# A transformer trunk on one core: when weight units are split, and where the pre-norm's mean stands, in the first blocks of each phase

## The chip, the cores and the metric

The kernel runs on one core of one Trainium2 chip. The metric is the device time of one execution in microseconds (us), as the median of several runs. The kernel before takes 2264.59 us (three runs, 2262.05 to 2264.63).

## The reference

It computes one layer of a decoder trunk on 288 tokens: 256 of a prompt and 8 times 4 of samples that continue a stored state. The width is 2048, the FFN's inner width 5632.

```python
x = x + 0.5 * rmsnorm(swiglu(rmsnorm(x, g[0]), ffn1_w_in, ffn1_w_out), g[1])
m, sg, sh = hybrid_mixer(rmsnorm(x, g[2]), mix_w_in, ..., s_gla, s_hgrn)
x = x + rmsnorm(m, g[3])
x = x + 0.5 * rmsnorm(swiglu(rmsnorm(x, g[4]), ffn2_w_in, ffn2_w_out), g[5])
```

In the mixer one projection gives `q, k, v, a_lr, r` of a gated linear attention (GLA, four heads) and the inputs of a second recurrence (HGRN2, eight heads). The decay of GLA comes from the low-rank part: `log_sigmoid(a_lr @ gla_w_up + gla_b) / 16`. Both recurrences are `S_t = diag(a_t) S_{t-1} + k_t^T v_t`, `o_t = q_t S_t`, worked out in chunks: scores `q k^T` with the decays inside, and the states.

## The kernel before, in words

**Layout.** Activations lie transposed, features on the 128 partitions and 288 tokens in the free dimension: x is 16 tiles `x0` to `x15` of 128x288. The program is there twice, once as it runs and once more in a branch that these inputs don't take; only the first copy is spoken of.

**Precision.** Every large product is made of three matmuls on numbers split into a high and a low part: high x by high weight, low x by high weight, high x by low weight (lines 555 to 557). ScalarE makes the high part of x (`xh`) with the norm's gain in it, VectorE the low part (`xl`, line 273).

**Weights.** They are read in units of 512 KB, numbered through the whole program in the order of their use. A unit is loaded by SyncE's queue into one of three buffers (`raw269` is unit 269's), and then *split*: ScalarE copies it to `wh` (line 101), VectorE subtracts to `wl` (line 102). That is `part()`. There are four buffers for split units, so a unit can be split when TensorE has finished the one four places before; some units at the head of a phase have two more buffers. A raw buffer is asked for again once its unit is split. `W.ahead(most)` splits as many units as there is room for, `most` at most. `W.behind`, if it is set, names instructions of which the next call's instructions are to come after in the order of the schedule (`issue_after`). What stands on an engine is set by that order, and each engine runs its own in sequence.

**Blocks.** `block()` makes a 128x4 by 2048 product: four column tiles of 128 rows of output (`qk0_0` to `qk0_3`) in four banks, over 16 rows k of x. Two rows make a unit, so a block has eight. After each unit but the last `W.ahead(most)` is called. The last unit is taken column by column, so that the banks come free one after the other, and each is emptied by `evac`. `tick(k)`, called behind each row k, places other work.

**Heads of phases.** The first block of a phase runs while the previous phase's norm is still being applied to x. `update(k)` makes `y[k]` (line 528), `x[k]` (529) and the two parts of x for one k. It is called by `tick0` of class `PreNorm`, eight rows ahead in the mixer and the second FFN. For the first column of such a block the first four rows are instead made from the old x and the unscaled update (class `Fill`): TensorE takes them ahead of the sum of squares; `scaled()` and `total()` put them together in `fsum` (lines 514 and 517). The second block, `v0` or the first `up`, has `tick1`: it squares x tiles (ScalarE) and adds them to `acc` (VectorE, line 417), and at k == 9 sets up the new norm: TensorE's `pre` (the mean, a product with a constant, line 444), a root on ScalarE, a reciprocal on VectorE (446), and what waited for it (`late`): in the mixer the scaling of `q_g`, `k_g`. The block's evacuations multiply by the reciprocal `rt`.

On TensorE `pre` stands in the middle of row 10 of that second block.

The mixer's blocks come in the order `qk0` (units 264 to 271), `v0` (272 to 279), `qk1` (280 to 287), `v1`. Between `v0` and `qk1` stands the head of the decay: `a_lr` (32 small matmuls, lines 1601 to 1605) and `gla_decay`, which multiplies by the gate's weights (`zp`, line 1612), and takes logarithms. The transposes of v's four tiles (`tp_v`, from `y8` to `y11`, line 939) are `turns`, taken one at a time by `tick` in `qk1`; `later` is a list of functions of which each tick takes one. The scan's scores (`sc`) then need the decayed keys `k_g`.

Of the kernel before, what the change touches and what calls it, by code (L numbers as in the profile page):

```python
# [13 lines left out]
ALU = mybir.AluOpType  # L14
# [129 lines left out]
def trunk(ctx, tc, x_prompt, x_sample, state_gla, state_hgrn, norm_gains, f1_in, f1_out, f2_in, f2_out,  # L144
# [3 lines left out]
    V, S, G, PE = nc.vector, nc.scalar, nc.gpsimd, nc.tensor  # L148
# [16 lines left out]
    def order(ins, before):  # L165
        tc.add_manual_dep(ins, before.name, mybir.DependencyInfo(mybir.DependencyClass.NoSync,
                                                                 mybir.DependencyReason.DATA), reason="act table")
# [16 lines left out]
    def mmtile(name):  # L184
        return mmp.tile([P, 512], F32, name=name, tag="mm")

    def auxtile(name):
        return aux.tile([P, 512], F32, name=name, tag="aux")


    W = Weights(tc, rawp, hlp)
# [132 lines left out]
    def x_copy(k, tp):  # L324
        return S.activation(x[k], tp, AF.Copy).ins if k % 2 else V.tensor_copy(x[k], tp).ins
# [4 lines left out]
    def after(ins, f, *args):  # L330
        with ExitStack() as es:
            for i in (*chain["pin"], *ins):
                es.enter_context(tc.issue_after(i))
            chain["pin"] = f(*args)
        return chain["pin"]
# [73 lines left out]
    def sq_add(src, k, pool=0, late=KT, n=KT):  # L409

        sq = acc if k == 0 else sqp.tile([P, T], F32, name="sq", tag="sq")
        if k < late:
            ins = S.activation(sq, src, AF.Square).ins
        else:
            ins = V.tensor_tensor(sq, src, src, op=ALU.mult).ins
        if 0 < k < n:
            (G if k < pool else V).tensor_tensor(acc, acc, sq, op=ALU.add)
        return sq, ins
# [21 lines left out]
    def rstd(dst, parts, name):  # L440

        ms = auxtile(name)
        for i, part in enumerate(parts):
            PE.matmul(ms[:, 0:T], onesD, part, start=i == 0, stop=i == len(parts) - 1)
        act(dst, ms[:, 0:T], AF.Sqrt, bias=epst)
        return V.reciprocal(dst, dst).ins

    class PreNorm:
# [6 lines left out]
        def tick0(self, k):  # L455
            if k + self.ahead < KT:
                self.split = self.update(k + self.ahead)

        def tick1(self, k):
            if k < 8:  # L460
                with tc.issue_after(self.split[0]), tc.issue_after(self.split[1]):
                    for j in (2 * k, 2 * k + 1):
                        sq_add(x[j], j)
            if k == 9:
                ins = rstd(rt, (acc,), self.name)

                behind = [G.memset(gate[:, 0:1], 0.0).ins, V.tensor_copy(gate[:, 1:2], epst).ins,
                          S.activation(gate[:, 2:3], epst, AF.Copy).ins]
                with ExitStack() as es:
                    for i in behind:  # L470
                        order(i, ins)
                        es.enter_context(tc.issue_after(i))
                    for f in self.late:
                        f()

    class Fill:
# [37 lines left out]
            V.tensor_tensor(self.sum, self.sum, self.scale[:, 0:T], op=ALU.mult)  # L514

        def total(self, ps):
            V.tensor_tensor(self.sum, self.sum, ps, op=ALU.add)
            return self.sum

    def post_norm(gcol, gnext, lasts, name, fill):  # L520
# [25 lines left out]
    def block(name, nk, rhs, evac, width=512, tick=None, tail=1, hold=False, most=99, fill=None, made=None):  # L546

        nf, per = width // P, 1024 // width
        nu = nk // per
        ps = [mmtile(f"{name}_{f}") for f in range(nf)]  # L550
        ws = [W.next() for _ in range(EARLY // per)] if fill else []

        def mm3(dst, w, f, k, parts, start, stop):
            c = (k % per) * width + f * P
            yield lambda: PE.matmul(dst, w[0][:, c:c + P], parts[0], start=start, stop=False)  # L555
            yield lambda: PE.matmul(dst, w[0][:, c:c + P], parts[1], start=False, stop=False)  # L556
            yield lambda: PE.matmul(dst, w[1][:, c:c + P], parts[0], start=False, stop=stop)  # L557

        def row(w, k):

            rows = [list(mm3(ps[f][:, 0:T], w, f, k, rhs(k), k == 0, False)) for f in range(nf)]
            made.extend(row[0]().ins for row in rows)
            if k == 0:
                after(made[-1:], second)
                after((), lambda: (x_copy(1, tps[1]), x_copy(0, tps[0])))
            with tc.issue_after(first.last if k == 0 else made[-1]):
                made.extend(row[i]().ins for i in (1, 2) for row in rows)

        def mm(w, f, k):
            if made is not None and k < 3:  # L570
                if f == 0:
                    row(w, k)
            elif not fill or f or k >= EARLY:
                for ready in mm3(ps[f][:, 0:T], w, f, k, rhs(k), k == 0, k == nk - 1):
                    ins = ready().ins
                    if made is not None:
                        made.append(ins)

        if fill:
            fill.products(lambda dst, k, parts, stop: mm3(dst, ws[k // per], 0, k, parts, k == 0, stop), ps[0][:, 0:T])  # L580
        for u in range(nu - tail):
            w = ws.pop(0) if ws else W.next()
            for k in range(u * per, (u + 1) * per):
                for f in range(nf):
                    mm(w, f, k)
                if tick is not None:
                    tick(k)
            W.ahead(most)
            if fill and u == 5:
                fill.scaled()  # L590
        ws = [W.next() for _ in range(tail)]
        for f in range(nf):
            for k in range((nu - tail) * per, nk):
                mm(ws[k // per - (nu - tail)], f, k)
            evac(f, fill.total(ps[f][:, 0:T]) if fill and f == 0 else ps[f][:, 0:T])
        for k in range((nu - tail) * per, nk):
            if tick is not None:
                tick(k)
        if not hold:
            W.ahead()  # L600
# [227 lines left out]
    def mixer(pn, border):  # L828
        with ExitStack() as mx:
# [103 lines left out]
            def group_tiles(nm):  # L933
                return {n: gp.tile([P, 2, T], F32, name=f"{n}_{nm}", tag=n) for n in ("q", "k", "f")}
# [40 lines left out]
            def log_sigmoid(out, z):  # L975

                e = tmp.tile([P, T], F32, name="ls", tag="ls")
                S.activation(e, z, AF.Abs)
                act(e, e, AF.Exp, scale=-1.0)
                act(e, e, AF.Ln, bias=1.0)  # L980
                V.scalar_tensor_tensor(out, z, 0.0, e, op0=ALU.min, op1=ALU.subtract)
# [579 lines left out]
            gens, later = [], []  # L1561
# [46 lines left out]
            def gla_decay(d, g):  # L1608
                for f in range(2):
                    a = 2 * g + f  # L1610
                    zp = auxtile("zp")
                    PE.matmul(zp[:, 0:T], aw[g][:, f * P:(f + 1) * P], alr, start=True, stop=True)
                    z = tmp.tile([P, T], F32, name="z", tag="z")
                    V.tensor_scalar(z, zp[:, 0:T], prm[:, 96 + a:97 + a], None, op0=ALU.add)
                    log_sigmoid(d["f"][:, f, :] if blockwise else z, z)
                    if not blockwise:
                        act(d["f"][:, f, :], z, AF.Exp, scale=1.0 / 16.0)
# [24 lines left out]
            for g in range(2):  # L1642
                d = group_tiles(f"g{g}")
                block(f"qk{g}", KT, xrhs, ev_gla(d, g == 0), tick=tick if g else pn.tick0, most=99 if g else 1,
                      fill=None if g else border.fill)
                if g == 0:
                    scan_pool()
                vt = vtiles(f"g{g}")
                if g == 0:
                    block("v0", KT, xrhs, ev_v(*vt), tick=pn.tick1)  # L1650
                    lower_bounds()
                    a_lr()
                    gla_decay(d, g)
                else:
                    gla_decay(d, g)
                    block("v1", KT, xrhs, ev_v(*vt), tick=tick)
                gens.append((g, (block_scan if blockwise else scan)(d, *vt, True, 4 * g, state_gla[0][:, 2 * g:2 * g + 2],
                                     sgp[0, 0, 2 * g:2 * g + 2], sgs[0][:, 2 * g:2 * g + 2]), True))
# [92 lines left out]
    u, border = ffn(1, lambda k: hg1[:, k:k + 1], 2, pn, first)  # L1751
    u, border = mixer(PreNorm("pre2", u, UPDATED), border)
# [45 lines left out]
```

## Time and profile before

| | |
|---|---|
| three runs | 2264.59 us median, 2262.05 to 2264.63 |
| the profiled execution, own time | 2262.32 us |
| its span | 2260.6 us |
| granted TensorE clock, mean | 0.999 |
| TensorE busy | 2247.0 us, 99% |
| VectorE busy | 1363.3 us, 60% |
| ScalarE busy | 1005.0 us, 44% |
| GpSimd busy | 78.3 us, 3% |

The span is the profiled time from the first to the last instruction; the execution's own time is 1.7 us longer. All times within the program are counted from the span's start. Matmuls are pipelined: the end of one is modelled, and the next starts before it.

### The profile page before, as it was taken

The page shows a single profiled execution, that of the slowest core. Times are in us where ns is not written, and L with a number is a line of the kernel's source. Part 1 is how long each engine was busy: PE and PEld are TensorE (multiplying, and loading weights), DVE is VectorE, ACT ScalarE, POOL GpSimd, SP SyncE. Part 2 cuts the span into 40 slices and gives each one's busy share as a digit, 9 for nine tenths or more (in the row PEclk, how much of TensorE's full clock was granted, in tenths as well). Part 3 has the DMA queues.
Part 4 walks back from the last instruction along what each step waited for, and adds up shares of the span by engine and source line. Part 5 has one row for each costly group of instructions (what it writes and reads, how often), then busy time and mean ns, then how long its engine had stood idle before and what let it go on. Part 6 is the DMA issues. An engine that isn't in the chain of part 4 may idle for free.

```text
span 2260.6 us, 41346 instructions
## 1 busy us (share of the span) xinstructions
PE 2247.0 (99%) x17075; PEld 2228.9 (99%) x17075; DVE 1363.3 (60%) x2166; ACT 1005.0 (44%) x1509; POOL 78.3 (3%) x143
## 2 busy tenths in 40 slices
PE   9999999999999999999999999999999999999998
PEld 9999999999999999999999999999999999999998
DVE  7545545554565468778788755844555455545545
ACT  6443333333334344545566644544333343333345
POOL 0000000000000003022110000100000000000000
PEclk9999999999999999999999999999999999999999
DMA  6555555555555555466565664555555555555553
GB/s 212 167 168 167 162 167 167 168 163 166 166 168 179 169 166 161 128 216 201 172 170 166 175 185 123 169 168 167 164 165 167 168 160 167 164 165 166 168 163 113
DMA packets 207330, 377.94 MB, mean 167 GB/s; under 512 B 15410, under 2 KB 40992, under 8 KB 207136
## 3 DMA queue, kind: packets, MB, share of 16 engines
q1 hardware_dynamic: 198832, 356.83, 52.8%
q0 software_dynamic: 5984, 17.97, 2.6%
q8 instruction: 135, 2.21, 0.4%
q10 hardware_dynamic: 2320, 0.44, 0.1%
q14 instruction: 59, 0.48, 0.1%
HBM read 363.39 MB, written 11.80 MB: 166 GB/s over the span
## 4 chain that ended last, share of the span: by engine, by line
PE 96%; DVE 2%; DMA 1%; ACT 1%; issue 1%; SPq 0%; DVEq 0%; ACTq 0%
PE gate L555 10%; PE gate L556 10%; PE gate L557 10%; PE out L556 8%; PE out L557 8%; PE out L555 8%; PE up L557 8%; PE up L555 8%; PE up L556 8%; PE mo L557 2%; PE mo L555 2%; PE mo L556 1%; PE hfq L555 1%; PE hfq L556 1%; PE hfq L557 1%; PE hi L555 1%
## 5 line engine op out<-in xcount | busy, mean ns | idle before, releaser
L102 DVE TENSOR_TENSOR wl<-raw,wh 128x1024 fp32r<-128x1024 f32 (+1 forms) x674 | 821.7, 1220 | 646.1 <-ACT wh L101 643.7
L101 ACT ACTIVATE wh<-raw 128x1024 fp32r<-128x1024 f32 (+1 forms) x673 | 710.7, 1057 | 1056.0 <-PE gate L556 313.0
L556 PE MATMUL gate<-xl,wh 128*128 128x288 f32 x1660 | 488.2, 295 | 0.1
L555 PE MATMUL gate<-xh,wh 128*128 128x288 f32 x1660 | 488.1, 297 | 0.2 <-ACT xh L272 0.2
L557 PE MATMUL gate<-xh,wl 128*128 128x288 f32 x1660 | 487.9, 295 | 0.0
L556 PE MATMUL out<-hl,wh 128*128 128x288 f32 x1408 | 416.2, 296 | 0.0
L555 PE MATMUL out<-hh,wh 128*128 128x288 f32 x1408 | 415.7, 295 | 0.0
L557 PE MATMUL up<-xh,wl 128*128 128x288 f32 x1408 | 415.5, 295 | 0.0
L557 PE MATMUL out<-hh,wl 128*128 128x288 f32 x1408 | 415.3, 295 | 0.0
L556 PE MATMUL up<-xl,wh 128*128 128x288 f32 x1408 | 415.3, 295 | 0.0
L555 PE MATMUL up<-xh,wh 128*128 128x288 f32 x1408 | 415.0, 295 | 0.0
L556 PEld LDWEIGHTS gate<-xl,wh 128*128 128x128 f32 x1660 | 311.7, 188 | 1.2 <-DVE xl L273 0.7
L555 PEld LDWEIGHTS gate<-xh,wh 128*128 128x128 f32 x1660 | 310.4, 188 | 1.2 <-ACT xh L272 0.7
L557 PEld LDWEIGHTS gate<-xh,wl 128*128 128x128 f32 x1660 | 311.3, 188 | 0.0
L555 PEld LDWEIGHTS out<-hh,wh 128*128 128x128 f32 x1408 | 265.0, 188 | 0.0
L557 PEld LDWEIGHTS out<-hh,wl 128*128 128x128 f32 x1408 | 264.9, 188 | 0.0
L556 PEld LDWEIGHTS out<-hl,wh 128*128 128x128 f32 x1408 | 264.8, 188 | 0.0
L557 PEld LDWEIGHTS up<-xh,wl 128*128 128x128 f32 x1408 | 264.5, 188 | 0.1
L556 PEld LDWEIGHTS up<-xl,wh 128*128 128x128 f32 x1408 | 264.4, 188 | 0.1
L555 PEld LDWEIGHTS up<-xh,wh 128*128 128x128 f32 x1408 | 264.3, 188 | 0.1
L704 DVE TENSOR_TENSOR y<-out,y 128x288 f32<-128x288 f32 x287 | 121.0, 452 | 103.7 <-PE out L557 100.8
L555 PE MATMUL hfq<-xh,wh 128*128 128x288 f32 x256 | 78.0, 305 | 0.0
(383 smaller groups left out, 2403.4 us busy)
## 6 DMA issues: line engine op xcount, KB each, us to landing
raw<-in_ffn_w_in_dram SPq DMA_DIRECT2D x351, 512.0 KB, 3.7
raw<-in_ffn_w_out_dram SPq DMA_DIRECT2D x176, 512.0 KB, 3.7
raw<-in_mix_w_in_dram SPq DMA_DIRECT2D x64, 512.0 KB, 3.7
raw<-in_mix_w_in_dram SPq DMA_DIRECT2D x96, 256.0 KB, 3.5
raw<-in_mix_w_out_dram SPq DMA_DIRECT2D x32, 512.0 KB, 3.7
out_dram<-s POOLq DMA_DIRECT2D x32, 256.0 KB, 3.5
s<-in_state_gla_dram POOLq DMA_DIRECT2D x16, 256.0 KB, 4.8
s<-in_state_hgrn_dram POOLq DMA_DIRECT2D x16, 256.0 KB, 4.5
```

The source lines that it names most:

```text
L101: i1 = self.nc.scalar.activation(h[:, c], raw[:, c], AF.Copy).ins
L102: i2 = self.nc.vector.tensor_tensor(l[:, c], raw[:, c], h[:, c].bitcast(F32), op=ALU.subtract).ins
L555: yield lambda: PE.matmul(dst, w[0][:, c:c + P], parts[0], start=start, stop=False)
L556: yield lambda: PE.matmul(dst, w[0][:, c:c + P], parts[1], start=False, stop=False)
L557: yield lambda: PE.matmul(dst, w[1][:, c:c + P], parts[0], start=False, stop=stop)
L704: V.tensor_tensor(y[k], ps, y[k], op=ALU.add)
```

## The change

It has five edits.

1. In `tick0`, for the phases that update x ahead (`made is None`), the next splits come behind ScalarE's instruction for the high part of the x tile that was last updated.
2. In `tick1` the mean is set up at k == 11 instead of k == 9.
3. `total()` makes the next splits come behind the first column's sum.
4. In a block with `fill`, the splits behind the first and the seventh unit are left out, and behind the others one unit is split, also where `most` was larger. Other blocks are as before.
5. In the mixer `gla_decay(d, 0)` does not follow `a_lr` directly but is put on `later` as the third of three functions, the first two of which do nothing: it is called at the third tick of `qk1`.

```diff
--- before.py
+++ after.py
@@ -455,13 +455,15 @@
         def tick0(self, k):
             if k + self.ahead < KT:
                 self.split = self.update(k + self.ahead)
+                if self.made is None:
+                    W.behind = self.split[:1]
 
         def tick1(self, k):
             if k < 8:
                 with tc.issue_after(self.split[0]), tc.issue_after(self.split[1]):
                     for j in (2 * k, 2 * k + 1):
                         sq_add(x[j], j)
-            if k == 9:
+            if k == 11:
                 ins = rstd(rt, (acc,), self.name)
 
                 behind = [G.memset(gate[:, 0:1], 0.0).ins, V.tensor_copy(gate[:, 1:2], epst).ins,
@@ -514,7 +516,7 @@
             V.tensor_tensor(self.sum, self.sum, self.scale[:, 0:T], op=ALU.mult)
 
         def total(self, ps):
-            V.tensor_tensor(self.sum, self.sum, ps, op=ALU.add)
+            W.behind = [V.tensor_tensor(self.sum, self.sum, ps, op=ALU.add).ins]
             return self.sum
 
     def post_norm(gcol, gnext, lasts, name, fill):
@@ -585,7 +587,10 @@
                     mm(w, f, k)
                 if tick is not None:
                     tick(k)
-            W.ahead(most)
+            if not fill:
+                W.ahead(most)
+            elif 0 < u < nu - tail - 1:
+                W.ahead(1)
             if fill and u == 5:
                 fill.scaled()
         ws = [W.next() for _ in range(tail)]
@@ -1650,7 +1655,7 @@
                     block("v0", KT, xrhs, ev_v(*vt), tick=pn.tick1)
                     lower_bounds()
                     a_lr()
-                    gla_decay(d, g)
+                    later.append([lambda: None, lambda: None, lambda d=d: gla_decay(d, 0)])
                 else:
                     gla_decay(d, g)
                     block("v1", KT, xrhs, ev_v(*vt), tick=tick)
```

`fsum`'s lines and others behind the first edit have numbers higher by 2 to 5 in the changed kernel (line 517 is 519, 1594 is 1599).

On VectorE, at the end of `qk0` and the start of `v0`, the rows from the split of 272 to that of 275 are these before (`wl` is a low part, `fsum` the first column's sum, `q_g0` and `k_g0` what the columns are copied to):

```order
L102 TENSOR_TENSOR wl272_9489<-raw272_9360,wh272_9488 128x1024
L273 SCALAR_TENSOR_TENSOR xl14_160<-x14_112,prm_94,xh14_144 128x288
L273 SCALAR_TENSOR_TENSOR xl15_161<-x15_113,prm_94,xh15_145 128x288
L102 TENSOR_TENSOR wl273_9519<-raw273_9392,wh273_9518 128x1024
L514 TENSOR_TENSOR fsum_9524<-fsum_9524,post1s_9278 128x288
L102 TENSOR_TENSOR wl274_9552<-raw274_9430,wh274_9551 128x1024
L517 TENSOR_TENSOR fsum_9524<-fsum_9524,qk0_0_9265 128x288
L1594 COPY q_g0_9262<-qk0_1_9266 128x288
L1594 COPY q_g0_9262<-fsum_9524 128x288
L1594 COPY k_g0_9263<-qk0_2_9267 128x288
L1594 COPY k_g0_9263<-qk0_3_9268 128x288
L102 TENSOR_TENSOR wl275_9587<-raw275_9492,wh275_9586 128x1024
```

and in the changed kernel:

```order
L102 TENSOR_TENSOR wl271_9459<-raw271_9237,wh271_9458 128x1024
L102 TENSOR_TENSOR wl272_9489<-raw272_9386,wh272_9488 128x1024
L516 TENSOR_TENSOR fsum_9524<-fsum_9524,post1s_9278 128x288
L417 TENSOR_TENSOR acc_164<-acc_164,sq_9619 128x288
L519 TENSOR_TENSOR fsum_9524<-fsum_9524,qk0_0_9265 128x288
L1599 COPY q_g0_9262<-qk0_1_9266 128x288
L102 TENSOR_TENSOR wl273_9519<-raw273_9424,wh273_9518 128x1024
L1599 COPY q_g0_9262<-fsum_9524 128x288
L1599 COPY k_g0_9263<-qk0_2_9267 128x288
L1599 COPY k_g0_9263<-qk0_3_9268 128x288
L102 TENSOR_TENSOR wl274_9581<-raw274_9462,wh274_9580 128x1024
L102 TENSOR_TENSOR wl275_9587<-raw275_9492,wh275_9586 128x1024
```

The split of 273 now stands between the copy of `qk0_1` and those of `fsum` and `qk0_2`, where it stood ahead of all of them, and that of 274 moves behind the four copies. Further up, the splits of 269, 270 and 271 move from behind x8, x11 and x13 to behind x12, x15 and `xl15`.

On TensorE, at the end of `v0`, where `v0_3` is the block's last column, the order before is

```order
L556 MATMUL v0_3_9605<-xl15_161,wh279_9768 128x288
L557 MATMUL v0_3_9605<-xh15_145,wl279_9769 128x288
L1605 MATMUL a_lr_9975<-x0_98,a32_9254 32x288
L1605 MATMUL a_lr_9975<-x1_99,a32_9254 32x288
L1605 MATMUL a_lr_9975<-x2_100,a32_9254 32x288
L1605 MATMUL a_lr_9975<-x3_101,a32_9254 32x288
```

and in the changed kernel

```order
L558 MATMUL v0_3_9605<-xl15_161,wh279_9768 128x288
L559 MATMUL v0_3_9605<-xh15_145,wl279_9769 128x288
L944 MATMUL tp_v_10024<-ident_84,y8_122 128x128 x2
L945 MATMUL tp_v_10024<-ident_84,v3_9930 96x128
L944 MATMUL tp_v_10051<-ident_84,y9_123 128x128 x2
L945 MATMUL tp_v_10051<-ident_84,v3_9939 96x128
L1610 MATMUL a_lr_9975<-x0_98,a32_9254 32x288
L1610 MATMUL a_lr_9975<-x1_99,a32_9254 32x288
```

The transposes of `y8` and `y9` and of their `v3` (the sample tokens' part) stood behind the second and the third row of `qk1` and are now ahead of `a_lr`. `zp`, which had five matmuls of `qk1` between `a_lr` and itself, now stands behind three rows of `qk1`, 36 matmuls. `pre` moves from the middle of row 10 of `v0` to the end of its row 11, 17 matmuls later; 48 matmuls of `v0` are left behind it.

On VectorE, behind the mean, the rows from the split of 280 on are these before (`gate`, `sel`, `hgain` and `a32` are small set-ups of the mixer, `rt` the reciprocal):

```order
L102 TENSOR_TENSOR wl280_9856<-raw280_9686,wh280_9855 128x1024
L446 RECIPROCAL rt_162<-rt_162 128x288
L467 COPY gate_93<-epst_91 128x1
L917 TENSOR_TENSOR sel_9253<-ident_84 128x32
L922 TENSOR_SCALAR hgain_9252<-prm_94 128x3
L1595 SCALAR_TENSOR_TENSOR q_g0_9262<-q_g0_9262,rt_162 128x288
```

and in the changed kernel:

```order
L102 TENSOR_TENSOR wl280_9800<-raw280_9686,wh280_9799 128x1024
L102 TENSOR_TENSOR wl281_9887<-raw281_9729,wh281_9886 128x1024
L446 RECIPROCAL rt_162<-rt_162 128x288
L469 COPY gate_93<-epst_91 128x1
L922 TENSOR_TENSOR sel_9253<-ident_84 128x32
L927 TENSOR_SCALAR hgain_9252<-prm_94 128x3
L1600 SCALAR_TENSOR_TENSOR q_g0_9262<-q_g0_9262,rt_162 128x288
```

The split of 281 now stands ahead of the reciprocal. In both kernels the other scalings of `q_g0` and `k_g0` follow, then a split (of 281 before, of 282 in the changed kernel), and then `y8`, the scaling of v's first column (line 960).

## Rows read from the trace of the kernel before

**Rows 1.** Page, the span and the busy line

```profile
span 2260.6 us, 41346 instructions
...
PE 2247.0 (99%) x17075; PEld 2228.9 (99%) x17075; DVE 1363.3 (60%) x2166; ACT 1005.0 (44%) x1509; POOL 78.3 (3%) x143
```

**Rows 2.** Timeline, TensorE, mixer's head: start us, us, instruction, [idle before <-releaser]

```profile
874.92 0.56 PE L555 MATMUL qk<-xh,wh 128*128 128x288 f32 x3
...
887.62 0.40 PE L555 MATMUL v<-xh,wh 128*128 128x288 f32 x1 [0.81 <-DVE fsum L517]
...
889.95 0.61 PE L555 MATMUL v<-xh,wh 128*128 128x288 f32 x1 [1.01 <-DVE k_g L1594]
...
893.23 0.30 PE L555 MATMUL v<-xh,wh 128*128 128x288 f32 x1
...
905.55 0.29 PE L555 MATMUL v<-xh,wh 128*128 128x288 f32 x1
906.47 0.73 PE L444 MATMUL pre<-acc,onesD 128*128 128x288 f32 x2 [0.64 <-DVE acc L417]
```

**Rows 3.** Windows: window, us, busy PE, PEld, DVE, ACT, POOL, granted clock, DMA share, GB/s

```profile
890.00:893.30 3.30, 3.30 (x14) 3.30 (x15) 2.22 (x4) 0.73 (x1) 0.00 (x0) 0.52 0.32 71
```

**Rows 4.** Timeline, second FFN's head: TensorE at the mean, VectorE at a copy

```profile
1443.36 0.72 PE L444 MATMUL pre<-acc,onesD 128*128 128x288 f32 x2 [0.47 <-DVE acc L417]
...
1427.65 0.30 DVE L629 COPY g<-fsum 128x288 f32<-128x288 f32 x1
```

**Rows 5.** Timeline, VectorE in qk0 and behind it

```profile
867.03 0.50 DVE L529 SCALAR_TENSOR_TENSOR x<-y,hg,x 128x288 f32<-128x288 f32 x1
...
868.88 1.22 DVE L102 TENSOR_TENSOR wl<-raw,wh 128x1024 fp32r<-128x1024 f32 x1
...
870.02 0.95 DVE L273 SCALAR_TENSOR_TENSOR xl<-x,prm,xh 128x288 fp32r<-128x288 f32 x2
870.88 0.52 DVE L529 SCALAR_TENSOR_TENSOR x<-y,hg,x 128x288 f32<-128x288 f32 x1
871.31 0.82 DVE L528 TENSOR_TENSOR y<-y,post1s 128x288 f32<-128x288 f32 x2
...
887.85 1.69 DVE L1594 COPY q_g<-fsum 128x288 f32<-128x288 f32 x1
```

**Rows 6.** Page, DMA issues: count, KB each, median us to landing

```profile
raw<-in_mix_w_in_dram SPq DMA_DIRECT2D x64, 512.0 KB, 3.7
```

**Rows 7.** Chain that ended last: start us, us, what

```profile
878.20 6.58 DMA raw<-in_mix_w_in_dram
```

**Rows 8.** Timeline, GpSimd at the mixer's head

```profile
872.08 4.95 POOL L1295 DMA_DIRECT2D s<-in_state_gla_dram  x7 [12.42 <-PE qk L556]
...
883.91 3.85 POOL L906 DMA_DIRECT2D y<-in_gla_w_gate_up_dram  x8
888.01 0.76 POOL L911 MEMSET Dg<- 128x768 f32 x1
```

**Rows 9.** Timeline, ScalarE behind the mean

```profile
907.24 0.50 ACT L179 ACTIVATE rt<-pre,epst 128x288 f32<-128x288 f32 x1 [0.61 <-PE pre L444]
```

**Rows 10.** Timeline, VectorE behind the mean

```profile
907.80 1.95 DVE L446 RECIPROCAL rt<-rt 128x288 f32<-128x288 f32 x1
...
911.86 1.22 DVE L102 TENSOR_TENSOR wl<-raw,wh 128x1024 fp32r<-128x1024 f32 x1
...
913.46 0.42 DVE L960 TENSOR_TENSOR y<-v,rt 128x256 f32<-128x256 f32 x1 [0.26 <-PE v L557]
```

**Rows 11.** Timeline, TensorE behind v0 and at the first scores

```profile
915.75 2.15 PE L1605 MATMUL a_lr<-x,a 128*32 128x288 f32 x32
...
918.59 1.19 PE L1612 MATMUL zp<-y,y 128*128 128x288 f32 x4
...
936.18 0.59 PE L1393 MATMUL sc<-q_g,k_g 128*128 128x256 f32 x2
```

**Rows 12.** Timeline, VectorE at the decayed keys

```profile
930.18 0.75 DVE L1348 TENSOR_TENSOR k_g<-k_g,f_g 128x576 f32<-128x576 f32 x1
```

## The prediction

> **What bounds the kernel now.** I began with the page's busy line: TensorE is busy for 2247.0 of 2260.6 us [rows 1]. So only time that TensorE loses can be won. Then I asked for the list of TensorE's waits. Apart from the start and one later score they lie in two places: the head of the mixer (the blocks `qk0` and `v0`, 854 to 916 us) and the up block at the head of the second FFN (1443 us).
>
> In the mixer's head one matmul of 288 columns follows another every 0.1325 us when nothing is late: 93 steps from 893.23 to 905.55 [rows 2]. From 874.92 (row k=10 of `qk0`) to the mean's matmul at 906.47 there are 199 matmuls, so 26.4 us of work in 31.55 us: 5.2 us are lost. The reader finds most of it in the same rows: 0.81 us for the total of the first tile, 1.01 for the copies of `qk0` out of their banks, and 0.64 for `acc`, the sum of squares; a smaller wait for the last x tiles is not shown. Each such figure is 0.16 short, since a matmul's modelled end lies 0.295 after its start. Behind the third wait the rows of `v0` stand 0.24 apart, and the stretch 890 to 893.3 has a granted clock of 0.52, the 1.2 GHz level, with 14 matmuls in 3.30 us where 1.86 would do [rows 3]: 1.44 us that the waits cost afterwards. In the second FFN's head only the wait for `acc` is left, 0.47 + 0.16 = 0.6 us [rows 4]. In the first FFN's head the mean waits for nothing (the list has nothing there). All that this change can win is thus 5.2 + 0.6 = 5.8 us, 0.26% of 2264.59. The kernel's three runs lie 2.6 us apart; about 0.2% (4.5 us) is what a measurement can tell from no change.
>
> **Part 1: the splits move behind x's tiles.** VectorE is the late engine in `qk0`. A tile of x costs it 1.22 us (0.36 for y, 0.43 each for x and `xl`), a weight split 1.14 [rows 5]. Before, units 269 to 273 are split between the tiles. Now 269 stands behind x12. I count its place from x7's update at 867.0: twelve steps of 0.43 and four of 0.36 give 873.6, so the split of 269 ends at 874.8, in time for k=10 at 874.9. Five steps and three y's later that of 270 ends at 879.2, and TensorE, which now runs four columns' high products first, needs it at 874.9 + 2 x 1.59 + 8 x 0.1325 = 879.1: 0.2 us lost with the semaphore (0 to 0.3). The split of 271 ends at 881.2, wanted at 881.3. `qk0` ends at 884.7; the wait for the last x tiles is gone.
>
> What is late next is the DMA. There are three raw slots, so the request of unit 272 waits for the split of 269, now 874.9 instead of 870.1, and that of 273 for the split of 270, 879.3. A unit lands in 3.7 us as a rule [rows 6] but took 6.58 [rows 7] when the mixer's states, requested at 872 to 877 [rows 8], were being loaded beside it. For 272 I take 5.8 (the states are in the queue throughout), so 880.7, split by 883.0; the sum, the total and the copy of column 1 follow by 884.6. So the total comes when TensorE comes to the second column of `v0`: the 0.81 is gone too. For 273 I take 4.6, between the ends, because most of the state bytes are in by then: 883.9, high part 885.0, low part 886.2. The changed order puts this split ahead of the copies of `fsum` and of column 2. They take 0.4 each, so column 2's bank is free at 887.1. TensorE is at the fourth column of `v0` (which needs that bank) ten matmuls after 884.7, at 886.0: a wait of 1.1, with the restart 1.2 us. With 3.7 for the DMA it is 0.2, with 6.58 it is 3.1. The half clock behind 889.95 goes if this wait stands alone, as I assume.
>
> **Part 2: the mean two rows later.** The squares are summed as before, by 906.4 at the latest (the mean started then); the mean's place is 17 matmuls later, so the waits of 0.64 and 0.47 go. But what hangs on the mean is 2.3 us later against the end of the block. Call the start of the mean's matmul t. ScalarE must first split unit 281 (the order puts it ahead of the root; its buffer is free at t): t + 0.3 to 1.3. Then the root, which before began 0.77 after the mean [rows 2, 9]. VectorE's split of 281 runs to t + 2.5 and holds the reciprocal. From the reciprocal's start to the next split before lie 4.06 us [rows 10]; that split is 1.14, then comes `y8`: t + 7.7 to 8.1. TensorE reaches the transposes of `y8`, which the new order puts ahead of `a_lr`, at t + 0.35 + 48 x 0.1325 = t + 6.7. Before, `y8` was begun at 913.46 [rows 10] and its transposes came far behind `a_lr` at 915.75 [rows 11]. With `v3`, `y9` and `v3` still to follow, `a_lr` starts at t + 9.0 rather than t + 7.4: a new wait of 1.6 us (1.3 to 2.0, by how soon ScalarE gets the buffer).
>
> The heads of the two FFNs have no transposes there. The first evacuation of the up block is reached by the same sum at t + 7.2, and the next block's second column asks for that bank at about t + 7.1: 0.2 us in each (0 to 0.5).
>
> **Part 3: the first decay in the next block.** `zp` began at 918.59, 0.7 us after `a_lr` (915.75, 2.15 long), and now comes behind its third row, 36 matmuls or 4.8 us in. The decayed keys were ready at 930.93 and the scores ran at 936.18 [rows 11, 12]: 5.2 us of cover. The move takes 4.0 of it, one split more that now stands in that chain 1.14, and the scores' turn comes 0.5 sooner as two transposes moved ahead: a wait of about 0.5 (0 to 1.1).
>
> **At nothing.** The splits left out behind the first and seventh units are made by the block's last call, which is unchanged: as many splits and requests in all. The splits of `fill2x` in the first FFN move behind its products; nobody reads them for 790 us.
>
> **The sum.** Won 5.8; new 0.2 + 1.2 + 1.6 + 0.5 + 0.2 + 0.2 = 3.9. That is -1.9 us on the profiled run, 2262.32 (span 2260.6): 2260.4. The median of the runs shown is 2.3 above that run, so I forecast 2264.6 - 1.9 = 2262.7.
>
> **Rivals.** *The clock drops behind a new wait.* The trace shows it behind 0.81 and 1.01 close together, not behind 0.64 alone. At 1.44 each, one drop gives 2264.1, two 2265.6. The Trainium skill ("TensorE: Matmul & The Clock Gate", section "What's actually happening") says that the throttled state is the default and activity releases it; the 0.52 behind the two waits agrees.
>
> *The copy of `fsum` stays slow.* At 887.85 it took 1.69 us [rows 5], its like in the second FFN 0.30 [rows 4]. GpSimd was then running its sets of `Dg` and their neighbours [rows 8]; at 886.2 it will still be issuing the eight loads before them (883.91 to 887.76). Beside loads the trace shows no such copy, so its price lies between 0.3 and 1.7. I take 0.4, since nothing is shown to block it there; 1.7 puts the wait at 2.5 and the time at 2264.0. The Trainium skill ("SBUF — State Buffer", section "Who interferes with whom") holds that a copy in a two-port mode and a GpSimd instruction shut each other out, whichever comes second waiting. By that rule a load being issued could hold the copy as the sets did; the slow copy beside them agrees, and for loads no row here decides.
>
> *Slower: the decay chain.* If the keys come 5 us after the scores' turn instead of 0.5, because ScalarE takes logarithms and splits in a worse order, the wait of 5 and a half clock add 5.9: 2268.6, and 2269.1 from 0.5 us more. It turns the change into a loss from a wait of 2.4 on. Against it stands the 5.2 of cover.
>
> *Nothing new waits.* The DMA in 3.7 us and a score chain without loss leave 0.2 + 1.6: -4.0, 2260.6. If the transposes are covered too it is 2258.8, which is more than 0.2%.
>
> *The change doesn't do what it says:* the freed VectorE time only moves the waits to 273's load, 3.1 rather than 1.2 us: 2264.6.
>
> **How the numbers follow.** Forecast 0.42; clock 0.18; slow copy 0.13; waits only moved 0.09; nothing new waits 0.10, of which 0.07 beyond 0.2%; decay chain 0.08, of which 0.07 beyond. So faster 0.07, same 0.86, slower 0.07. The range leaves out the two ends: from -4.3 (the best case without the transposes' full 1.6) to +2.2 (two clock drops and the slow copy), 2260.3 to 2266.8.
>
> **What would show it.** Right: no wait for x's high part or for `acc` in the heads; one wait of TensorE of about a microsecond for the copy of column 2 near 886 us; a wait of 1.3 to 1.6 for `y8` behind `v0`; a granted clock of 1 all through. Wrong: the load of unit 273 landing before 883 or after 885, a copy of `fsum` over a microsecond, a clock of 0.5 behind either wait, or a wait for the scores over 1.1 us.

## The result, and the profile after

The changed kernel takes 2264.69 us (median of 22 runs, 2261.70 to 2268.52), the kernel before 2261.32 (22 runs, 2258.77 to 2264.63, the three shown above among them). The ratio is 1.0016, 95% interval 1.0009 to 1.0022: it is slower by 3.4 us, or 2 to 5. A gain of 1.9 was forecast. The profiled execution after took 2264.74, close to its median; the one before, 2262.32, is 1.0 above its median.

The page of the changed kernel, which answers to [rows 1]:

```profile
span 2263.0 us, 41353 instructions
...
PE 2247.3 (99%) x17075; PEld 2228.8 (98%) x17075; DVE 1362.1 (60%) x2166; ACT 1006.4 (44%) x1509; POOL 78.5 (3%) x143
```

The same work, 2.4 us more of span. TensorE's timeline in the mixer's head, the answer to [rows 2]:

```profile
885.97 0.29 PE L557 MATMUL v<-xh,wh 128*128 128x288 f32 x1
888.93 0.40 PE L557 MATMUL v<-xh,wh 128*128 128x288 f32 x1 [2.67 <-DVE k_g L1599]
...
893.21 0.30 PE L557 MATMUL v<-xh,wh 128*128 128x288 f32 x1
...
908.32 0.65 PE L444 MATMUL pre<-acc,onesD 128*128 128x288 f32 x2
...
916.29 0.44 PE L944 MATMUL tp_v<-ident,y 128*128 128x128 f32 x2 [0.96 <-DVE y L965]
...
938.25 0.70 PE L1398 MATMUL sc<-q_g,k_g 128*128 128x256 f32 x2 [0.99 <-DVE k_g L1353]
```

The reader finds the three new waits at the three places named in the prediction: the copy of a column of `qk0` ahead of `v0_3`, the scaling `y8` ahead of its transposes, the decayed keys ahead of the scores. The mean at 908.32 waits for nothing, and neither does the one in the second FFN. The first wait is more than twice as long as forecast. The granted clock in the stretches around it:

```profile
874.90:884.70 9.80, 9.72 (x72) 9.31 (x71) 9.23 (x17) 5.35 (x9) 9.80 (x25) 1.00 0.95 290
884.70:889.80 5.10, 2.43 (x18) 2.19 (x17) 3.53 (x6) 3.44 (x4) 5.10 (x12) 1.00 0.67 186
889.80:893.20 3.40, 3.40 (x16) 3.40 (x15) 2.88 (x5) 1.43 (x3) 1.75 (x4) 0.50 0.77 242
```

In the third stretch it is 0.50, as in [rows 3], behind one long wait instead of two short ones. The chain of waits says what came late first; the columns are start, length, what:

```profile
879.32 5.84 DMA raw<-in_mix_w_in_dram
885.27 1.07 ACT wh L101
```

and VectorE's timeline goes on from there, and shows the places of the two later waits:

```profile
886.36 1.23 DVE L102 TENSOR_TENSOR wl<-raw,wh 128x1024 fp32r<-128x1024 f32 x1 [1.57 <-ACT wh L101]
887.50 1.02 DVE L1599 COPY q_g<-fsum 128x288 f32<-128x288 f32 x1
888.44 0.80 DVE L1599 COPY k_g<-qk 128x288 f32<-128x288 f32 x2
...
914.68 1.22 DVE L102 TENSOR_TENSOR wl<-raw,wh 128x1024 fp32r<-128x1024 f32 x1
915.82 0.41 DVE L965 TENSOR_TENSOR y<-v,rt 128x256 f32<-128x256 f32 x1
...
936.31 1.22 DVE L102 TENSOR_TENSOR wl<-raw,wh 128x1024 fp32r<-128x1024 f32 x1
937.45 0.75 DVE L1353 TENSOR_TENSOR k_g<-k_g,f_g 128x576 f32<-128x576 f32 x1
```

Three times a weight split stands directly ahead of the instruction for which TensorE waits. The first of them itself waits 1.57 us, since its unit, 273, landed at 885.2.

### The profile page after: what moved, and what is told of

Same layout as the page of the kernel before. It is cut to its first block, busy times and chain, and to the rows that moved or that the text cites. A ratio compares the mean times of both kernels' runs of the same rounds, so it can differ in the third digit from the quotient of the medians.

```text
span 2263.0 us, 41353 instructions
## 1 busy us (share of the span) xinstructions
PE 2247.3 (99%) x17075; PEld 2228.8 (98%) x17075; DVE 1362.1 (60%) x2166; ACT 1006.4 (44%) x1509; POOL 78.5 (3%) x143
## 4 chain that ended last, share of the span: by engine, by line
PE 95%; DVE 3%; DMA 1%; ACT 0%; issue 0%; ACTq 0%; SPq 0%; DVEq 0%
PE gate L557 10%; PE gate L559 10%; PE gate L558 10%; PE out L558 8%; PE up L559 8%; PE up L557 8%; PE out L559 8%; PE up L558 8%; PE out L557 8%; PE mo L559 2%; PE mo L557 1%; PE mo L558 1%; PE hfq L557 1%; PE hfq L558 1%; PE hfq L559 1%; PE v L557 1%
```

## The experiments

Each ratio is to the kernel before, timed beside it on the same chip.

| run | median, us | ratio, 95% interval |
|---|---|---|
| splits alone | 2264.37 | 1.0015, 1.0005 to 1.0024 |
| mean alone | 2261.94 | 1.0005, 0.9996 to 1.0014 |
| decay alone | 2261.93 | 1.0006, 0.9997 to 1.0015 |
| changed, 273 behind the copies | 2260.80 | 1.0002, 0.9993 to 1.0011 |
| splits alone, 273 behind the copies | 2261.44 | 1.0004, 0.9995 to 1.0013 |
| the same, mean at k == 10 | 2258.42 | 0.9989, 0.9980 to 0.9998 |
| changed, mean at k == 10 | 2263.94 | 1.0012, 1.0002 to 1.0021 |
| changed, decay behind `a_lr` | 2265.68 | 1.0017, 1.0008 to 1.0026 |
| changed, state loads held back | 2261.84 | 1.0005, 0.9996 to 1.0014 |
| 273 behind the copies, k == 10, state loads held back | 2258.71 | 0.9989, 0.9980 to 0.9998 |

### Each part by itself

The splits alone, against the changed kernel:

```diff
-            if k == 11:
+            if k == 9:
...
-                    later.append([lambda: None, lambda: None, lambda d=d: gla_decay(d, 0)])
+                    gla_decay(d, g)
```

> Only the edits to the splits (1, 3 and 4); the mean at k == 9 and the decay behind a_lr as before. Theory A (the loss is a sum of three new waits, one of each part, of which this part only moves time): VectorE's split of 273 still stands ahead of the copies that free qk0's banks and waits for its load, TensorE loses 2 to 3 us at the fourth column of v0, the clock is half from 889.8 to 893.2, and the wait for acc stays (0.6); 0 to 1 us slower than before. Rival B (the whole loss comes from the splits): 2.5 to 4 us slower. Rival C (the splits win and the other two parts lose): 1 to 3 us faster.

TensorE's timeline of that run, and its windows around a second fall of the clock (of which more in the last section):

```profile
886.03 0.40 PE L557 MATMUL v<-xh,wh 128*128 128x288 f32 x1 [0.70 <-DVE fsum L519]
...
889.69 0.47 PE L557 MATMUL v<-xh,wh 128*128 128x288 f32 x1 [2.48 <-DVE k_g L1599]
...
907.07 0.72 PE L444 MATMUL pre<-acc,onesD 128*128 128x288 f32 x2 [0.47 <-DVE acc L417]
```

```profile
1394.00:1398.40 4.40, 4.40 (x39) 4.40 (x38) 2.51 (x4) 1.77 (x4) 0.00 (x0) 1.00 0.26 101
1398.50:1401.80 3.30, 3.30 (x16) 3.30 (x16) 0.18 (x1) 0.24 (x1) 0.00 (x0) 0.50 0.55 164
```

It measured 3.4 us slower than before, by the ratio (1.1 to 5.4): rival B of that run. Each wait is as theory A has it, but the sum isn't: the splits alone are as slow as the whole change. Of what this profile lost against the first one of before, 2.3 us lie in the second FFN's head: the second fall of the clock, which no other trace has, and 0.97 instead of 0.47 for `acc`. Theory A compared with the first profile of before, and what follows shows that this profile was no fair base.

The mean alone and the decay alone, against before:

```diff
-            if k == 9:
+            if k == 11:
```

```diff
-                    gla_decay(d, g)
+                    later.append([lambda: None, lambda: None, lambda d=d: gla_decay(d, 0)])
```

> Only the mean at k == 11. Theory A: the waits for acc (0.64 in the mixer, 0.47 in the second FFN) go and no transposes stand ahead of a_lr, since it is the decay's move that puts them there: 0.5 to 1.6 us faster. Rival B: the later reciprocal makes TensorE wait for y8 or for the first evacuation all the same: same to 1.5 us slower, with a wait of over 0.5 us at a_lr or in qk1.

> Only the decay moved to qk1's third tick. Theory A: two rows' time of cover is gone, so the first scores wait 0 to 1 us for the decayed keys; the transposes of y8 stand ahead of a_lr but y8 is there in time, since the mean is early: 0 to 1.2 us slower. Rival B (the scores' wait in the changed kernel came from the later mean alone): no wait at the scores, 0.2 us either way.

The mean alone has a new wait at `zp`, for VectorE's scaling of `a_lr`:

```profile
916.73 1.24 PE L1612 MATMUL zp<-y,y 128*128 128x288 f32 x4 [1.89 <-DVE y L1606]
```

So rival B holds for it: `acc`'s two waits are gone, and 1.9 us come back one step later. With the decay alone:

```profile
886.73 0.40 PE L555 MATMUL v<-xh,wh 128*128 128x288 f32 x1 [1.24 <-DVE fsum L517]
...
903.16 0.72 PE L444 MATMUL pre<-acc,onesD 128*128 128x288 f32 x2 [0.64 <-DVE acc L417]
...
934.26 0.70 PE L1393 MATMUL sc<-q_g,k_g 128*128 128x256 f32 x2 [0.75 <-DVE k_g L1348]
```

The scores wait 0.75 with the mean early, so theory A holds. Both times lie within what can be told from no change. But these two kernels have before's order in `qk0` and the first rows of `v0`, and neither shows the waits and the half clock of [rows 2, 3].

### The same kernels once more

Both kernels as they are, for another profile of each; nothing is edited.

> The kernel before, a second look at the mixer's head. Theory A (what it lost there in its first profile, 0.8 and 1.0 us and the half clock, was large by chance, since the runs with the mean alone and with the decay alone have the same order up to the mean and lost 0.2 and 1.4): 0.2 to 2 us lost between the second half of qk0 and v0's fourth row, and no half clock. Rival B (4 us are lost there as a rule): both waits and the half clock come again.

> The changed kernel, a second look. Theory A: the wait at v0's fourth column comes again with 2.3 to 3 us and the half clock behind it, the transposes wait 0.9 to 1.2, the first scores 0.8 to 1.1, and the HGRN scores near 1109 us about 1. Rival B (these are chance as well): two of the four differ by over 0.7 us from the first look.

The kernel before, second profile: TensorE's timeline, ScalarE's around the split of 273 (its copy to `wh`, then the high parts of the last x tiles), and the row of the chain for the load of 274:

```profile
884.85 0.80 PE L555 MATMUL qk<-xh,wh 128*128 128x288 f32 x4 [2.30 <-ACT xh L272]
...
890.10 0.40 PE L555 MATMUL v<-xh,wh 128*128 128x288 f32 x1 [0.46 <-DVE fsum L517]
...
906.25 0.72 PE L444 MATMUL pre<-acc,onesD 128*128 128x288 f32 x2 [0.64 <-DVE acc L417]
```

```profile
883.32 1.06 ACT L101 ACTIVATE wh<-raw 128x1024 fp32r<-128x1024 f32 x1 [4.91 <-DMA raw<-in_mix_w_in_dram]
884.28 0.95 ACT L272 ACTIVATE xh<-x,prm 128x288 fp32r<-128x288 f32 x2
```

```profile
879.05 8.21 DMA raw<-in_mix_w_in_dram
```

The changed kernel, second profile:

```profile
888.01 0.40 PE L557 MATMUL v<-xh,wh 128*128 128x288 f32 x1 [1.41 <-DVE k_g L1599]
...
913.83 0.44 PE L944 MATMUL tp_v<-ident,y 128*128 128x128 f32 x2 [0.96 <-DVE y L965]
```

For the kernel before neither theory holds whole. Its long wait stood in another place (the last x tiles, 2.30) and had no half clock: the load of 273 took 7.75 us, ScalarE's split of it waited 4.91 for that, and the last two high parts stood behind the split. So a split that waits for its load holds up TensorE in this order too, on ScalarE. The load of 274, at 8.21, made the wait of 0.46. For the changed kernel rival B holds: the waits at the transposes and the scores came again (0.96 and 1.01), but the first was 1.41 without a half clock, and the one near 1109 us, which the first profile had with 1.07, was absent. To compare, the same stretch of matmuls in every trace, from one in `qk0` to the 116th of `v0` (in row 9), ahead of any mean; its 247 steps need 247 x 0.1325 = 32.73 us:

| trace | first start | last start | lost, us | half clock |
|---|---|---|---|---|
| before | 866.78 | 904.09 | 4.6 | yes |
| before, second profile | 867.62 | 903.86 | 3.5 | no |
| mean alone | 867.35 | 901.06 | 1.0 | no |
| decay alone | 866.03 | 900.78 | 2.0 | no |
| changed | 866.72 | 904.48 | 5.0 | yes |
| changed, second profile | 867.04 | 902.03 | 2.3 | no |
| splits alone | 866.67 | 905.25 | 5.9 | yes |
| changed, decay behind `a_lr` | 867.36 | 905.94 | 5.9 | yes |
| changed, mean at k == 10 | 866.43 | 904.78 | 5.6 | yes |
| changed, 273 behind the copies | 865.58 | 900.67 | 2.4 | no |
| splits alone, 273 behind the copies | 867.20 | 900.70 | 0.8 | no |
| the same, k == 10 | 867.13 | 902.25 | 2.4 | no |
| changed, state loads held back | 867.66 | 902.06 | 1.7 | no |
| 273 behind, k == 10, held back | 867.42 | 901.02 | 0.9 | no |

The first four have before's order in this stretch: 2.8 on average, from 1.0 to 4.6. The next five have the changed order: 4.9, four of them over 5. So the splits' part costs about 2.1 there, where the prediction had it win; with such a spread in so few traces the 2.1 is rough. (The four profiled executions lie 0.3 us below their kernels' medians on average, the five 0.6, so the choice of profiles does not make the difference.)

### The split of 273 behind the copies

```diff
-            elif 0 < u < nu - tail - 1:
+            elif 0 < u < nu - tail - 2:
...
-                        V.tensor_copy(dst, ps)
+                        W.behind = [V.tensor_copy(dst, ps).ins]
```

(and the same for the copies of the second FFN's first gate block), once in the changed kernel and once with the splits alone.

> The changed kernel with the split of 273 taken out of the rows of qk0 and put, with 274 and 275, behind the copy of the last column; the same in the second FFN. Theory A: the wait of 2.67 us at the fourth column of v0 goes and with it the half clock (1.44), but acc, which VectorE sums behind the splits, is now late at the mean by 0 to 2: 2.2 to 4.3 us faster than the changed kernel, so between 1 us faster and 1 us slower than before. Rival B (273's split now comes too late for row 2 of v0): a wait of about the same size for wl273, no more than 1 us faster than the changed kernel. Rival C (the clock falls at 889.8 whatever TensorE did): the half clock stays without a wait before it, 1.4 us less gain.

> The splits alone with the split of 273 behind the copies of qk0; mean at k == 9, decay behind a_lr. Theory A (in the splits' part the one costly place is 273's split ahead of the copies; the first run of the splits alone was 3.5 slower than before): the wait of 2.5 us at the fourth column of v0 and its half clock go, some 0.3 is left there, and 0.7 at the total and 0.5 to 1 at acc stay; no wait at the transposes, at zp, at the first scores; 3 to 5 us faster than the splits alone, so 0 to 2 us faster than before. Rival B (the splits behind x's tiles are late as such): no more than 1 us faster than the splits alone.

In the changed kernel the long wait is gone, and with it the half clock:

```profile
885.12 0.40 PE L557 MATMUL v<-xh,wh 128*128 128x288 f32 x1 [0.70 <-DVE fsum L519]
...
886.51 0.41 PE L557 MATMUL v<-xh,wh 128*128 128x288 f32 x1 [0.34 <-DVE k_g L1599]
```

2260.80 is 3.9 below 2264.69; by the ratios it is 3.2. That is theory A, and rivals B and C fall. With the splits alone the edit brings 2.9, or 2.5 by the ratios, a little under the 3 to 5 expected, and the result is no faster than before, where 0 to 2 us was expected. The head's gain runs into the mean at k == 9, in the mixer and in the second FFN:

```profile
903.36 0.72 PE L444 MATMUL pre<-acc,onesD 128*128 128x288 f32 x2 [1.85 <-DVE acc L417]
...
1442.06 0.72 PE L444 MATMUL pre<-acc,onesD 128*128 128x288 f32 x2 [0.83 <-DVE acc L417]
```

In the mixer the wait for `acc` was 0.47 in the slow head and 1.85 in the quick one; 0.5 of the difference is that `pre` stands four matmuls earlier here.

### The mean's rows and the decay's place

The mean at k == 10 in the last kernel, and in the changed kernel; and the changed kernel with the decay behind `a_lr` again:

> The same kernel with the mean at k == 10. Theory A: half of acc's wait goes (0.2 to 0.6 in each of the two heads), and zp, which waited 1.9 us for the reciprocal's followers with the mean at k == 11, waits under 0.8, as only one of the two rows of delay is there: 0.3 us faster to 0.5 us slower than with k == 9. Rival B: whatever acc gains zp loses at once: the sum of both waits within 0.3 us of that with k == 9.

> The changed kernel with one number changed: the mean at k == 10. Theory A (two rows are one too many: what follows the reciprocal is then late wherever the decay stands): the transposes' wait of 0.96 and most of the scores' wait of 1.0 go, acc waits 0 to 0.4; 1.3 to 2.2 us faster than the changed kernel, that is 1.2 to 2.3 slower than before. Rival B (the scores wait because the decay was moved): their wait stays at 0.8 or more and the gain is under 1.1.

> The changed kernel with the decay directly behind a_lr again, the mean at k == 11. Theory A: no transposes stand ahead of a_lr and the scores have their cover again, but zp waits some 1.9 us as in the run with the mean alone; within 0.7 us of the changed kernel. Rival B (the decay's move costs about 2 us by itself): 1.5 to 2.2 us faster than the changed kernel.

The first is the only order here, with the one below, that beats the kernel before clear of its interval: 2258.42, by 0.11%. Neither of its theories foresaw this: against k == 9 it is 3.0 us faster, or 3.4 by the ratios, where theory A had 0.3 faster to 0.5 slower. The two waits for `acc` explain the 3.0: 1.85 and 0.83, each 0.16 short, were all lost with k == 9, and here the mean waits for nothing in either head. Nor does `zp` wait, for which theory A allowed 0.8, nor the transposes or the first scores; up to there only waits in the head are left:

```profile
886.61 0.41 PE L557 MATMUL v<-xh,wh 128*128 128x288 f32 x1 [0.69 <-DVE fsum L519]
...
888.10 0.40 PE L557 MATMUL v<-xh,wh 128*128 128x288 f32 x1 [0.42 <-DVE k_g L1599]
...
904.60 0.72 PE L444 MATMUL pre<-acc,onesD 128*128 128x288 f32 x2
```

In the changed kernel the mean at k == 10 frees the transposes and the scores still wait 1.05, which is rival B's sign. The gain of 0.8 us is within its bound too, but the two intervals overlap, so the time does not tell the theories apart:

```profile
937.26 0.70 PE L1398 MATMUL sc<-q_g,k_g 128*128 128x256 f32 x2 [1.05 <-DVE k_g L1353]
```

With the decay behind `a_lr` and the mean at k == 11 the loss only changes its place. The time is the changed kernel's by the ratios (0.2 us apart; 1.0 by the medians, where theory A allowed 0.7), and the wait at `zp` is theory A's:

```profile
890.38 0.48 PE L557 MATMUL v<-xh,wh 128*128 128x288 f32 x1 [2.47 <-DVE k_g L1599]
...
921.61 1.24 PE L1617 MATMUL zp<-y,y 128*128 128x288 f32 x4 [1.89 <-DVE y L1611]
```

So with the decay early, the mean two rows later costs 1.9 at `zp`; with the decay late it costs 0.96 at the transposes, and the decay's move 0.75 to 1.05 at the scores. One row later with the decay early costs nothing, and behind the quick head it wins the 3.0 of `acc`.

### The state loads held back

```diff
                         t = sp[0].tile([P, nb, dv], F32, name="s0", tag="s0", bufs=8)
+                        if copied:
+                            V.tensor_copy(t[:, 0, 0:1], copied.pop()[:, 0:1])
```

(`copied` holds the last copy's destination.) GpSimd's state loads then start at 886 us or later instead of 872.

> The changed kernel with GpSimd's first state loads held back behind the copies of qk0 (the first state tile gets one column written by VectorE from k_g0, and the load writes over it). Theory A (the load of 273 is slow since the state loads lie beside it): it lands 3.7 to 4.4 us after its request instead of 5.8, the wait at v0's fourth column falls to 0.3 to 1.3 and no half clock follows; 1 to 3.5 us faster than the changed kernel, less 0 to 1 if the state loads now delay loads of qk1's weights. Rival B (273's load is slow for another reason, or its split waits for its buffers): the wait stays over 2 us.

> The run with the split of 273 behind the copies, the mean at k == 10 and the decay behind a_lr, which was 2.4 us faster than before, with the same state loads held back. Theory A: the load of 272 too lands 2 us sooner, so the waits of 0.69 at the total and 0.42 at the next column go: 0.5 to 1.5 us faster than without, 2.5 to 4 faster than before. Rival B (the state loads are in the way wherever they lie): as fast as without or slower, with a wait for a weight load in qk1 or a late state at the samples.

In the changed kernel:

```profile
888.04 0.40 PE L557 MATMUL v<-xh,wh 128*128 128x288 f32 x1 [0.92 <-DVE k_g L1601]
...
914.36 0.44 PE L944 MATMUL tp_v<-ident,y 128*128 128x128 f32 x2 [1.45 <-DVE y L965]
```

The wait falls from 2.67 to 0.92, no half clock follows, and 2.9 us are won (2.5 by the ratios), as theory A has it. Unit 272 landed in 3.6 us instead of 6.1, unit 273 in 4.8 instead of 5.8, where 3.7 to 4.4 was expected. So the state loads account for about 1.0 of the 1.75 us by which this wait is shorter; the other 0.7 is the copy of `fsum`, 0.30 us here and 1.02 there. The transposes wait longer, 1.45 instead of 0.96; VectorE waits 0.39 there for a small load of ScalarE's queue. In the best order the windows show a head in which next to nothing is lost, the DMA share at 0.53 where the changed kernel had 0.95:

```profile
874.90:884.90 10.00, 10.00 (x74) 9.59 (x74) 10.00 (x19) 5.27 (x10) 7.33 (x16) 1.00 0.53 147
884.90:893.20 8.30, 8.18 (x61) 7.94 (x61) 7.88 (x11) 5.47 (x8) 2.31 (x6) 1.00 0.77 243
```

and yet 2258.71 is no faster than the 2258.42 without it. The profiled execution took 2257.90 here; without the loads held back it took 2259.93, which is 1.5 above that kernel's median. So in most of its executions the kernel without it lost less than its profile shows. Theory A's gain of 0.5 to 1.5 on top is not there. Rival B has the time right, but not its waits: in this trace the other seven state loads are asked for from 914.6 us on, and TensorE waits for nothing from the head to the second recurrence, where every trace has a wait of 0.6. Why the two kernels take the same time stays open.

## Why the prediction was wrong

Two steps failed, the budget and the size of the new wait in Part 1. In the head ahead of the mean the prediction had 4.4 us won and 1.4 new (0.2 + 1.2), so 3.0 won; the traces have 2.1 lost. Of these 5.1 us the budget is 1.6 and Part 1 is 3.5.

**The budget.** The step that failed first is "Won 5.8": it counted every wait of one profiled execution as there in each. Of the 5.2 in the mixer's head, 4.1 (0.47, 0.97, 1.17 and the half clock) hang on when two or three weight loads land among the state loads, and on whether the copy of `fsum` then meets GpSimd's sets (1.69 us there, 0.30 to 0.71 in the other three traces). Both change from run to run: in four traces with this order 4.6, 3.5, 1.0 and 2.0 us were lost in the same stretch. What the splits' part could remove was 2.8 at the mean, not 4.6.

**Part 1, what is late next.** The mechanism was right and named: 273's split ahead of the copies of `fsum` and of column 2, behind its load. Up to there the working held: unit 272 landed at 880.9 (880.7 was said), its split ended at 883.3 (883.0), and `v0` began at 884.8 (884.7). The size of the wait was not right: 1.2 was said, the five traces show 2.67, 1.41, 2.48, 2.47 and 3.23, and 4.9 us were lost in the stretch where 1.4 was said. What makes the first longer is the load (5.84 where 4.6 was taken "because most of the state bytes are in by then": 1.2) and the copy of `fsum` (1.02 where 0.4 was taken: 0.6). In the two traces with 2.48 and 2.47 the copy stood beside GpSimd's sets and took 1.38 and 1.89, which the rival of the slow copy had with a wait of 2.5. And "the half clock goes if this wait stands alone, as I assume" failed: it came in four of the five, in two of them (2.67 and 3.23) behind this wait alone. The rival "waits only moved" was the nearest: it had the wait at 3.1, but no half clock beside it, and the rival of the clock had 1.44 but the wait at 1.2. Both came together.

**Part 2.** The waits for `acc` went as said, and the transposes' wait came: 0.96, with the restart 1.12, where 1.6 (1.3 to 2.0) was said. The mean's matmul began at t = 908.32 and `y8` at 915.82, t + 7.5, where t + 7.7 to 8.1 was said: ScalarE began the split of 281 at 908.39, t + 0.07, ahead of the 0.3 to 1.3 that was allowed. The reason given was incomplete: the runs show that the transposes stand there because the decay moved away, and that without its move the later mean costs more, 1.9 at `zp`.

**Part 3.** The wait for the scores was 0.99, with the restart 1.15, at the upper bound of "about 0.5 (0 to 1.1)"; the split that stands just ahead of the keys (936.31) is the "one split more" of the working. The chain did not reach the 2.4 of the slower rival.

**The sum by rows.** The splits' part +2.1 in the head (table); `acc` -0.8 and in the second FFN -0.6; transposes +1.12; scores +1.15; the two FFNs' heads +0.2 and +0.3, by how much further apart the starts in the two profiles stand 100 matmuls later: +3.5, against 3.4 measured. The head's averages rest on four and five traces that spread over 3.6 us each, so the agreement is better than the method. By the same rows the splits alone come to about +2.4 (the head's 2.1, `acc` -0.2 in the mixer and +0.5 in the second FFN), where 3.4 was measured; how the loss divides among the parts is known to about 1 us. The wait near 1109 us (0.8 to 1.3 in six of the fourteen traces, in kernels with and without the moved decay, in one of two traces of the changed kernel) is left out of it; whether the change makes it likelier stays open.

**The level.** 2262.7 was forecast and 2264.69 measured, which lies in the range only because the forecast was counted from 2264.6. Over 22 runs before's median is 2261.32; counted from there the forecast would have been 2259.4 and the range 2257.0 to 2263.5. That the measured time fell into the range, and next to the 2264.6 of "waits only moved", is luck.

## What to carry to other kernels

A wait that one profile shows behind a load among other loads is one draw: look at the same stretch in other executions, or in kernels that share its order, before it is counted as something to win. When a split, a cast or any other work that needs a load is moved, see what stands behind it on its engine: here it was the copies that free TensorE's banks, and moving one split behind them won 2.5 to 3.2 us by the ratios, though the result beat the kernel before only when the mean came one row later as well. And a step off a busy engine's path (the mean) can be moved later only as far as its followers have cover: one row cost nothing and won 3.0 us once the work ahead of it was quick, two cost 1.9 us.

## What the runs showed of the hardware

**The clock.** The half clock came in five of the fourteen heads, each time for 3.41 us: during or up to 0.9 us behind waits of 0.81 and 1.01, of 2.67, of 3.23, of 0.70 and 2.48, and of 0.69 and 2.47. It did not come behind a single wait of 2.30, nor behind 1.41. The Trainium skill ("TensorE: Matmul & The Clock Gate", section "What's actually happening") says that the throttled state is the default and that activity releases it; the falls behind waits agree. In the run with the splits alone the half clock came once more at 1398.45 us with no wait at all: the windows above have TensorE busy for all of the 4.40 us before. Its last work there included 18 matmuls of one column each for the post-norm's mean. The same 18 stand in the other thirteen traces without a fall, so what set this one off stays open.

**The copy and GpSimd.** The copy of `fsum`, from SBUF to SBUF, took 0.30 us in four traces and 0.55 to 2.02 in the other ten. In the last run of the table, VectorE and then GpSimd:

```profile
884.07 0.44 DVE L1601 COPY q_g<-qk 128x288 f32<-128x288 f32 x1
884.43 2.02 DVE L1601 COPY q_g<-fsum 128x288 f32<-128x288 f32 x1
886.38 0.44 DVE L1601 COPY k_g<-qk 128x288 f32<-128x288 f32 x1
```

```profile
884.67 0.33 POOL L913 MEMSET a<- 128x256 f32 x1
884.92 0.76 POOL L916 MEMSET Dg<- 128x768 f32 x1
885.60 0.17 POOL L917 MEMSET Ds<- 128x64 f32 x1
885.69 0.60 POOL L921 MEMSET qm<- 128x576 f32 x1
886.22 0.28 POOL L926 CAST bmask<-bm 96x8 f32<-96x8 int32 x1
```

The copy ends as the row of sets ends, as it does in all five traces in which it stood beside that row (0.93 to 2.02 us, within 0.05 of the row's end), while the copies from the PSUM banks next to it take 0.44; the one ahead of it took 0.44 or 0.45 in all fourteen traces, whatever GpSimd did. The Trainium skill ("SBUF — State Buffer", section "Who interferes with whom") has a copy in a two-port mode and a GpSimd instruction shut each other out, the second waiting; the rows agree that the copy waits. On what the prediction left open, the copy beside the eight loads of the gate's weights that GpSimd was issuing took 0.30 in two traces and 0.55 to 1.02 in five.
